# adaLN column sums turned by full transposes, and the final norm's weights transposed earlier, in a one-core hybrid layer

## The chip, the core and the metric

The kernel runs on one NeuronCore of a Trainium2 chip. The metric is device time in microseconds (us) of one execution. The engines named below are TensorE (PE in the profile, with its weight loads apart as PEld), VectorE (DVE), ScalarE (ACT), GpSimd (POOL) and the queue of SyncE (SP), which issues the weight transfers.

## What is computed

One decoder layer for 256 tokens of width 1024, in float32. A conditioning vector c gives nine rows of 1024 numbers (adaLN): shift, scale and gate for each of three sub-layers. The reference, cut to what matters here:

```python
ada = jax.nn.silu(c) @ w_ada[l] + b_ada[l]
sh1, sc1, g1, sh2, sc2, g2, sh3, sc3, g3 = jnp.split(ada, N_ADA, axis=-1)
h = modulate(rmsnorm(x, norm_ffn1[l]), sh1, sc1)
x = x + 0.5 * g1[:, None, :] * swiglu(h, w_ffn1_in[l], w_ffn1_out[l])
...
y_att = moba_attention(...)
y_ssm = s5_mixer(...)
x = x + g2[:, None, :] * (merged @ w_out[l])
h = modulate(rmsnorm(x, norm_ffn2[l]), sh3, sc3)
x = x + 0.5 * g3[:, None, :] * swiglu(h, w_ffn2_in[l], w_ffn2_out[l])
return rmsnorm(x, norm_final)
```

## The kernel before

Activations lie transposed (features on partitions). Each weight element is split in two fp32r parts: ACT casts the high part (`w_hi`, line 271), DVE subtracts it to get the low part (`w_lo`, line 279), and PE makes three passes for each product (lines 302 to 304, and 475 to 477 for the output projections). Weight tiles of 1 MB come through four `raw` buffers; `nextq` hands out the split halves in order and counts them in `state["q"]`, and four buffers of each part are in use (`NSPLIT`).

The work runs in stages: FFN1 (to about 236 us), the projections of the mixing block, attention and the state-space scan (to about 372 us), the output projection, FFN2 (from about 424 us), the final norm. In the attention stage, sixteen gate units of 24 matmuls each (banks 4 to 6, lines 302 to 304) are the filler between the narrow pieces: scores (`L1249`, `L1250`), softmax on DVE and ACT (`L1263`, `L1269`, `L1274`), the transposes of the probabilities (`L1283`), their copies on ACT (`L1285`, `L1286`), the product with v (`L1302`, `L1304`), the state-space output (`L1223`) and its gelu on ACT (`L1234`). ACT loads one function table for gelu and another for the exponential.

The adaLN rows 2 to 8 of the nine (rows 0 and 1 go another way) are summed on DVE, as weight tiles arrive, into an accumulator of 128 x 1024, `acc` (line 251). When one is complete, `ada_done` puts a closure in the queue `pe_fill`; `fill`, called at fixed points of the stages, takes the first entry when `state["q"]` has reached its number. The closure sums over partitions with ones (`L378`, four products of 32 columns' weights, each quarter of the row then standing in 32 equal partitions), copies the 128 x 256 result to `ada_rows` (ACT, `L383`), turns it into columns on PE (`L385`) and adds bias on DVE (`ada_cols`). The seven closures run in the trace at 110.9, 154.8, 195.6, 287.9, 339.3, 372.0 and 550.2 us.

The weights of the final norm (8 x 128) are turned into columns by `final_gain` (`L1415` on PE, `L1416` on DVE), also from `pe_fill`; they are used only in the last stage, from 605.7 us. The order of instructions within an engine is set by a scheduler from the program and its own estimates, except in sections where the order is written out by hand.

Of the kernel before, what the change touches and what calls it, by code (L numbers as in the profile page):

```python
# [14 lines left out]
ALU = mybir.AluOpType  # L15
# [4 lines left out]
KD = D // 128  # L20
# [35 lines left out]
def kernel(ctx, tc, T, out):  # L56
    nc = tc.nc
# [33 lines left out]
    def bank(i):  # L91
        return psum.tile([128, 512], F32, tag=f"bank{i}", name=f"bank{i}")

    def sb(tag, shape, dt=F32, bufs=1, name=None):
        return parts[place.get(tag, "pool")].tile(shape, dt, tag=tag, name=name or tag, bufs=bufs)
# [127 lines left out]
    state = {"loaded": 0, "split": 0, "q": 0, "bank": 3}  # L223
# [4 lines left out]
    pe_fill = deque()  # L228
# [102 lines left out]
    ident = const.tile([128, 128], F32, name="ident")  # L331
# [9 lines left out]
    bada = cols0[:, 0:72].rearrange("p (v k) -> p v k", k=KD)  # L341
    ldt = const.tile([128, 16], F32, name="ldt")
    norm_cols = {1: cols0[:, 72:80], 4: cols[:, 32:40], 7: cols[:, 40:48]}
# [15 lines left out]
    ada = {v: const.tile([128, KD], F32, name=f"ada{v}") for v in range(9)}  # L359

    def ada_cols(v, p, ks):

        o, b = ada[v][:, ks], bada[:, v, ks]
        if v in norm_cols:
            nc.vector.scalar_tensor_tensor(out=o, in0=p, scalar=1.0, in1=b, op0=ALU.add, op1=ALU.add)
            nc.vector.tensor_tensor(out=o, in0=o, in1=norm_cols[v][:, ks], op=ALU.mult)
        else:
            nc.vector.tensor_tensor(out=o, in0=p, in1=b, op=ALU.add)
            if v % 3 == 2:
                nc.vector.tensor_scalar(o, o, 0.5, None, op0=ALU.mult)  # L370

    def ada_done(v):
        a = acc.pop(v)

        def do_cols():
            p = bank(state["bank"])
            for q in range(4):
                nc.tensor.matmul(  # L378
                    p[32 * q:32 * q + 32, 0:256], ones[:, 0:32], a[:, q * 256:(q + 1) * 256], start=True, stop=True,
                    tile_position=(0, 32 * q),  # L380
                )
            rs = sb("ada_rows", [128, 256])
            nc.scalar.copy(rs, p[:, 0:256])  # L383
            for n in range(2):
                nc.tensor.matmul(  # L385
                    p[:, 256 + n:264:2], rs[:, n * 128:(n + 1) * 128], ident[:, ::32], start=True, stop=True
                )
            ada_cols(v, p[:, 256:264], slice(0, KD))

        pe_fill.append((state["q"] + FILL_DELAY, do_cols))  # L390

# [16 lines left out]
    def ada_block_cols(b):  # L408
        a = block_sb.pop(b)
        p = bank(7)  # L410
        for n in range(2):
            nc.tensor.matmul(p[:, n:n + 1], a[:, n * 128:(n + 1) * 128], one1, start=True, stop=True)
        ks = slice(b, b + 1)
        ada_cols(1, p[:, 0:1], ks)
        ada_cols(0, p[:, 1:2], ks)
# [588 lines left out]
    start = ExitStack()  # L1004
# [26 lines left out]
    for j in range(1, 4):  # L1031
# [19 lines left out]
        out=sel, in_=sel, compare_op=ALU.is_equal, fill=0.0, base=0, pattern=[[-1, 2], [0, 64]], channel_multiplier=1  # L1051
# [93 lines left out]
    for j in range(4):  # L1145
        p = bank(4 + j)[:, 0:S]
# [3 lines left out]
        for n in range(4):  # L1150
            for t in range(4):
                o = U[32 * t:32 * t + 32, 4 * j + n, 1:NC4 + 1]
# [167 lines left out]
    for hd in range(8):  # L1320
        n = 2 * hd - (hd > 6)
# [11 lines left out]
    for n in range(16):  # L1333
        g, j = divmod(n, 8)
        p = bank(4 + n % 3)[:, 0:S]
# [34 lines left out]
    for q in range(4):  # L1370
        p = bank(4 + q)
# [7 lines left out]
    for q in range(4):  # L1379
        p = bank(4 + q)  # L1380
# [22 lines left out]
    ks = range(KD - HOLD, KD)  # L1403
# [11 lines left out]
        nc.tensor.transpose(p[:, 0:KD], rows[0], ident[0:8, 0:8])  # L1415
        nc.vector.tensor_copy(nf, p[:, 0:KD])  # L1416

    pe_fill.append((state["q"] + 30, final_gain))

    def each(g):  # L1420
        if g == 0:
# [37 lines left out]
    for t in range(2):  # L1459
        o = sb(("ssm_Pr", "ssm_Pi")[t], [128, D])  # L1460
# [37 lines left out]
```

## Time and profile before

| | us |
|---|---|
| median of 3 runs | 624.38 |
| lowest and highest of them | 622.92, 624.68 |
| profiled execution, its own time | 622.35 |
| its span, first to last instruction | 620.3 |
| PE busy | 601.8 (97%) |
| DVE busy | 456.6 (74%) |
| ACT busy | 327.5 (53%) |

The time of an execution is 2.05 us longer than its span. Busy time of PE counts pipelined matmuls, so two facts are read apart: how long PE had nothing to do, and the distance from the start of one matmul to the start of the next, which is what an instruction costs in a full stream.

### The profile page before, as it was taken

Reading aid. Unit: us, or ns where it says so; the run is one execution under the profiler, and the core shown is the slowest. Engines: PE = TensorE matmul, PEld = TensorE weight load, DVE = VectorE, ACT = ScalarE, POOL = GpSimd, SP = SyncE. Lnnn points to the kernel's source line nnn. Section 1 sums busy time; section 2 is a strip of 40 time slices with the busy share of each in tenths; the row PEclk is TensorE's granted clock in tenths of the full one; section 3 lists DMA queues with packets and bytes.
Section 4 is the critical chain, followed back from the end, with each engine's and each line's share of the span. In section 5 each row is a group of like instructions: output and inputs, shape, how many; then the busy total and the mean of one; then the engine's idle time right before and its main releaser. Section 6 shows DMA issues by size and latency. Waiting matters only on the chain.

```text
span 620.3 us, 12787 instructions
## 1 busy us (share of the span) xinstructions
PE 601.8 (97%) x5328; PEld 573.4 (92%) x5328; DVE 456.6 (74%) x838; ACT 327.5 (53%) x537; POOL 23.6 (4%) x37
## 2 busy tenths in 40 slices
PE   7999999999999998999999999997999999999996
PEld 6778999999999998998877899997999999999995
DVE  2699999899875577999998758865984646654533
ACT  5336856488434453756446865454744344434434
POOL 5200000020000001000000000001000000000000
PEclk9999999999999997999999999997999999999997
DMA  9999989866887645698337745574376755855301
GB/s 277 333 253 330 340 281 326 291 233 231 273 288 251 205 136 186 225 313 295 138 137 278 267 136 204 173 235 135 139 261 213 248 170 195 272 175 170 132 2 69
DMA packets 97706, 136.70 MB, mean 220 GB/s; under 512 B 7697, under 2 KB 77410, under 8 KB 97648
## 3 DMA queue, kind: packets, MB, share of 16 engines
q1 hardware_dynamic: 97360, 135.81, 65.7%
q8 instruction: 42, 0.69, 0.5%
q14 instruction: 16, 0.13, 0.1%
q0 software_dynamic: 288, 0.07, 0.1%
HBM read 134.82 MB, written 1.05 MB: 219 GB/s over the span
## 4 chain that ended last, share of the span: by engine, by line
PE 86%; DVE 7%; DMA 3%; ACT 1%; issue 1%; SPq 0%; POOLq 0%; DVEq 0%; ACTq 0%
PE bank L302 17%; PE bank L304 16%; PE bank L303 16%; PE bank L475 8%; PE bank L476 8%; PE bank L477 8%; PE bank L626 4%; DVE w_lo L279 2%; DMA raw<-in_w_ffn_in_dram 2%; DMA raw<-in_w_ada_dram 1%; PE bank L1223 1%; DVE ssm_U L1157 1%; PE bank L502 1%; PE bank L400 1%; DVE a L689 1%
## 5 line engine op out<-in xcount | busy, mean ns | idle before, releaser
L279 DVE TENSOR_TENSOR w_lo<-raw,w_hi 128x1024 fp32r<-128x1024 f32 (+1 forms) x184 | 221.4, 1210 | 90.7 <-ACT w_hi L271 90.2
L271 ACT CAST w_hi<-raw 128x1024 fp32r<-128x1024 f32 (+1 forms) x184 | 189.3, 1039 | 176.4 <-PE bank L303 106.3
L302 PE MATMUL bank<-h_hi,w_hi 128*128 128x256 f32 x736 | 208.2, 283 | 0.0
L304 PE MATMUL bank<-h_hi,w_lo 128*128 128x256 f32 x736 | 206.1, 280 | 0.8 <-DVE w_lo L279 0.7
L303 PE MATMUL bank<-h_lo,w_hi 128*128 128x256 f32 x736 | 205.9, 280 | 0.0
L302 PEld LDWEIGHTS bank<-h_hi,w_hi 128*128 128x128 f32 x736 | 138.6, 188 | 4.7 <-issue 2.8
L304 PEld LDWEIGHTS bank<-h_hi,w_lo 128*128 128x128 f32 x736 | 138.8, 189 | 1.7 <-DVE w_lo L279 1.1
L303 PEld LDWEIGHTS bank<-h_lo,w_hi 128*128 128x128 f32 x736 | 138.7, 188 | 0.1
L475 PE MATMUL bank<-a,w_hi 128*128 128x256 f32 x352 | 99.1, 282 | 0.0
L476 PE MATMUL bank<-a,w_hi 128*128 128x256 f32 x352 | 98.7, 280 | 0.0
L477 PE MATMUL bank<-a,w_lo 128*128 128x256 f32 x352 | 98.5, 280 | 0.0
L251 DVE SCALAR_TENSOR_TENSOR acc<-raw,csil,acc 128x1024 f32<-128x1024 f32 x49 | 62.7, 1280 | 7.8 <-DMA raw<-in_w_ada_dram 7.4
L475 PEld LDWEIGHTS bank<-a,w_hi 128*128 128x128 f32 x352 | 66.3, 188 | 1.0 <-issue 1.0
L477 PEld LDWEIGHTS bank<-a,w_lo 128*128 128x128 f32 x352 | 66.6, 189 | 0.0
L476 PEld LDWEIGHTS bank<-a,w_hi 128*128 128x128 f32 x352 | 66.4, 189 | 0.0
L302 PE MATMUL bank<-a,w_hi 128*128 128x258 f32 x128 | 38.8, 303 | 2.1 <-ACT w_hi L271 2.1
L303 PE MATMUL bank<-a,w_hi 128*128 128x258 f32 x128 | 38.2, 298 | 0.0
L304 PE MATMUL bank<-a,w_lo 128*128 128x258 f32 x128 | 37.2, 293 | 0.0
L626 PE MATMUL bank<-h_hi,w_hi 128*128 128x256 f32 x112 | 27.4, 292 | 1.2 <-ACT h_hi L452 0.8
L302 PEld LDWEIGHTS bank<-a,w_hi 128*128 128x128 f32 x128 | 26.0, 203 | 2.5 <-ACT w_hi L271 2.5
L626 PE MATMUL bank<-h_lo,w_hi 128*128 128x256 f32 x112 | 27.5, 284 | 0.0
L626 PE MATMUL bank<-h_hi,w_lo 128*128 128x256 f32 x112 | 27.3, 282 | 0.0
(323 smaller groups left out, 827.4 us busy)
## 6 DMA issues: line engine op xcount, KB each, us to landing
raw<-in_w_ffn_in_dram SPq DMA_DIRECT2D x36, 1024.0 KB, 5.2
raw<-in_w_ada_dram SPq DMA_DIRECT2D x28, 1024.0 KB, 5.3
raw<-in_w_ffn_out_dram SPq DMA_DIRECT2D x22, 1024.0 KB, 5.1
raw<-in_w_in_dram SPq DMA_DIRECT2D x16, 1024.0 KB, 6.4
raw<-in_w_ada_dram SPq DMA_DIRECT2D x16, 512.0 KB, 8.3
raw<-in_w_ffn_in_dram SPq DMA_DIRECT2D x8, 896.0 KB, 7.3
raw<-in_w_out_dram SPq DMA_DIRECT2D x4, 1024.0 KB, 4.9
raw<-in_w_br_att_dram SPq DMA_DIRECT2D x2, 1024.0 KB, 5.0
```

What stands on the lines that cost most here:

```text
L251: nc.vector.scalar_tensor_tensor(out=a, in0=r[:, k, :], scalar=cs, in1=a, op0=ALU.mult, op1=ALU.add)
L271: nc.scalar.copy(hi, r)
L279: nc.vector.tensor_tensor(out=lo, in0=r, in1=hi.bitcast(F32), op=ALU.subtract)
L302: nc.tensor.matmul(o, st[0], mv[0], start=first, stop=False)
L303: nc.tensor.matmul(o, st[0], mv[1], start=False, stop=False)
L304: nc.tensor.matmul(o, st[1], mv[0], start=False, stop=last)
L400: nc.tensor.matmul(p[q:q + 32, 0:256], csil[:, k, :], r[:, k, :], start=(k < 4), stop=(k >= 4), tile_position=(0, q))
L475: nc.tensor.matmul(mm3_o, wj[0], a[0], start=first and j % 2 == 0, stop=False)
L476: nc.tensor.matmul(mm3_o, wj[0], a[1], start=False, stop=False)
L477: nc.tensor.matmul(mm3_o, wj[1], a[0], start=False, stop=last and j % 2 == 1)
L502: nc.tensor.matmul(p[:, t:t + 1], z[:, t * 128:(t + 1) * 128], one1, start=(first and n == 0 and t == 0), stop=(last and n == len(parts) - ...
L626: nc.tensor.matmul(pb[b][:, n * S:(n + 1) * S], z[:, b * 128:(b + 1) * 128], h[hl][:, kb, :], start=(kb == 0 and n == 0 and y == 0), stop= ...
```

## The change

The two products that turn `ada_rows` into columns are replaced. Before, each used `ada_rows` as the stationary 128 x 128 operand and every 32nd column of the identity as the moving one (4 columns), and wrote 4 interleaved columns. Now each is a transpose of 128 x 128, whose 128 columns go to the upper half of the bank, and `ada_cols` reads every 32nd of them. And the number at which `final_gain` may run goes from 30 to 10 halves after the start of FFN2.

```diff
     def ada_cols(v, p, ks):
 
-        o, b = ada[v][:, ks], bada[:, v, ks]
+        o, b, g = ada[v][:, ks], bada[:, v, ks], norm_cols[v][:, ks] if v in norm_cols else None
+        if len(p.shape) == 3:
+            o, b, g = (z if z is None else z.rearrange("p (q n) -> p q n", n=2) for z in (o, b, g))
         if v in norm_cols:
             nc.vector.scalar_tensor_tensor(out=o, in0=p, scalar=1.0, in1=b, op0=ALU.add, op1=ALU.add)
-            nc.vector.tensor_tensor(out=o, in0=o, in1=norm_cols[v][:, ks], op=ALU.mult)
+            nc.vector.tensor_tensor(out=o, in0=o, in1=g, op=ALU.mult)
...
             for n in range(2):
-                nc.tensor.matmul(
-                    p[:, 256 + n:264:2], rs[:, n * 128:(n + 1) * 128], ident[:, ::32], start=True, stop=True
-                )
-            ada_cols(v, p[:, 256:264], slice(0, KD))
+                nc.tensor.transpose(p[:, 256 + n * 128:384 + n * 128], rs[:, n * 128:(n + 1) * 128], ident)
+            ada_cols(v, p[:, 256:512].rearrange("p (n q c) -> p q n c", n=2, q=4)[:, :, :, 0], slice(0, KD))
...
-    pe_fill.append((state["q"] + 30, final_gain))
+    pe_fill.append((state["q"] + 10, final_gain))
```

The scheduler also places some instructions of the attention stage differently. On ACT, in the stretch from about 342 to 356 us of the trace before, the row stood thus (`a_4529` is the output of gelu, its two rows the two halves of the second block; `at_e` the exponentials of a head, two rows each):

```order
247 L1234 ACT_TABLE_LOAD
248 L1234 ACTIVATE a_4529<-bank_4215 128x4x64
249 L1255 ACTIVATE at_bias<-dist 128x256
250 L1234 ACTIVATE a_4529<-bank_4215 128x4x64
251 L1341 ACTIVATE ssm_G_3657<-bank_4422 128x256
252 L271 CAST w_hi<-raw 128x1024
253 L1269 ACT_TABLE_LOAD
254 L1269 ACTIVATE at_e,at_st<-a_3699,at_st 128x128
255 L1269 ACTIVATE at_e,at_st<-a_3699,at_st 128x256
```

Now, on the same engine, from the same first table load on:

```order
247 L1234 ACT_TABLE_LOAD
248 L1234 ACTIVATE a_4529<-bank_4215 128x4x64
249 L1269 ACT_TABLE_LOAD
250 L1269 ACTIVATE at_e,at_st<-a_3699,at_st 128x128
251 L1269 ACTIVATE at_e,at_st<-a_3699,at_st 128x256
```

And nine rows further on, still on ACT:

```order
260 L1234 ACT_TABLE_LOAD
261 L1234 ACTIVATE a_4529<-bank_4215 128x4x64
262 L1269 ACT_TABLE_LOAD
263 L1269 ACTIVATE at_e,at_st<-a_3699,at_st 128x128
264 L1269 ACTIVATE at_e,at_st<-a_3699,at_st 128x256
```

The second half of that gelu has moved behind the exponentials of one head more, and two table loads have been added.

On PE, the transposes of the probabilities of the head whose exponentials are the last two of these rows (`bank_4562`) stood in the gate unit `bank_4586` thus:

```order
2434 L302 MATMUL bank_4586<-h_hi,w_hi 128x256
2435 L1283 MATMUL bank_4562<-ident,at_e 128x128
2436 L303 MATMUL bank_4586<-h_lo,w_hi 128x256
2437 L1283 MATMUL bank_4562<-ident,at_e 128x128 x2
2438 L304 MATMUL bank_4586<-h_hi,w_lo 128x256
```

Now, in the same unit, which begins at row 2431:

```order
2444 L303 MATMUL bank_4586<-h_lo,w_hi 128x256
2445 L1283 MATMUL bank_4562<-ident,at_e 128x128
2446 L304 MATMUL bank_4586<-h_hi,w_lo 128x256
2447 L302 MATMUL bank_4586<-h_hi,w_hi 128x256
2448 L1283 MATMUL bank_4562<-ident,at_e 128x128 x2
2449 L303 MATMUL bank_4586<-h_lo,w_hi 128x256
```

They stand behind fourteen matmuls of the unit instead of one.

On PE, at the beginning of FFN2, behind the second output step (`L477`) and ahead of the first input step (`L302`, `h_hi`), the rows now are:

```order
3161 L476 MATMUL bank_5643<-a_5312,w_hi 128x256
3162 L477 MATMUL bank_5643<-a_5312,w_lo 128x256
3163 L1415 MATMUL bank_5702<-ident,rows_96 128x8
3164 L302 MATMUL bank_5705<-h_hi,w_hi 128x256
3165 L303 MATMUL bank_5705<-h_lo,w_hi 128x256
```

Before, `L477` and `L302` were neighbours there, and `L1415` stood some 480 rows later. The order of POOL and of the DMA queue is unchanged.

## Rows read from the trace of the kernel before

**Rows 1.** The page, part 4: the chain that ended last, by engine.

```profile
PE 86%; DVE 7%; DMA 3%; ACT 1%; issue 1%; SPq 0%; POOLq 0%; DVEq 0%; ACTq 0%
```

**Rows 2.** Stretches: length, busy us (count) of PE, PEld, DVE, ACT, POOL; clock, DMA.

```profile
100.00:200.00 100.00, 100.00 (x917) 98.05 (x916) 83.05 (x128) 56.50 (x80) 3.69 (x3) 1.00 0.78 273
338.00:364.00 26.00, 26.00 (x259) 21.85 (x259) 17.95 (x42) 18.84 (x46) 0.00 (x0) 1.00 0.58 207
440.00:613.00 173.00, 173.00 (x1483) 171.96 (x1482) 101.36 (x116) 78.55 (x98) 0.00 (x0) 1.00 0.53 177
```

**Rows 3.** Groups by line: busy us, mean ns of one record, idle before.

```profile
L385 PE MATMUL bank<-ident,ada_rows 128*128 128x4 f32 x28 | 3.7, 239 | 0.1
L887 PE MATMUL bank<-ident,big 128*128 128x128 f32 x32 | 4.9, 274 | 0.0
```

**Rows 4.** Timeline of PE at the first closure: start, us, instruction.

```profile
110.77 0.28 PE L304 MATMUL bank<-h_hi,w_lo 128*128 128x256 f32 x1
110.88 0.55 PE L385 MATMUL bank<-ident,ada_rows 128*128 128x4 f32 x4
111.29 0.36 PE L302 MATMUL bank<-h_hi,w_hi 128*128 128x256 f32 x1
111.49 0.28 PE L303 MATMUL bank<-h_lo,w_hi 128*128 128x256 f32 x1
111.61 0.28 PE L304 MATMUL bank<-h_hi,w_lo 128*128 128x256 f32 x1
```

**Rows 5.** Timeline of PE around four transposes of line 887.

```profile
99.72 0.28 PE L477 MATMUL bank<-a,w_lo 128*128 128x256 f32 x1
99.83 0.60 PE L887 MATMUL bank<-ident,big 128*128 128x128 f32 x4
100.19 0.37 PE L302 MATMUL bank<-h_hi,w_hi 128*128 128x256 f32 x1
100.40 0.28 PE L303 MATMUL bank<-h_lo,w_hi 128*128 128x256 f32 x1
```

**Rows 6.** Timeline of PE around two transposes of line 1283.

```profile
350.85 0.37 PE L302 MATMUL bank<-h_hi,w_hi 128*128 128x256 f32 x1
351.06 0.38 PE L1283 MATMUL bank<-ident,at_e 128*128 128x128 f32 x2
351.19 0.36 PE L303 MATMUL bank<-h_lo,w_hi 128*128 128x256 f32 x1
351.39 0.28 PE L304 MATMUL bank<-h_hi,w_lo 128*128 128x256 f32 x1
```

**Rows 7.** Timeline of PE after the fourth closure, with the waits.

```profile
293.00 0.28 PE L302 MATMUL bank<-h_hi,w_hi 128*128 128x256 f32 x1
293.71 0.52 PE L1165 MATMUL bank<-ssm_U,ssm_G 128*128 128x64 f32 x3 [0.43 <-DVE a L689]
...
312.53 0.39 PE L304 MATMUL bank<-h_hi,w_lo 128*128 128x256 f32 x1 [0.71 <-DVE w_lo L279]
```

**Rows 8.** Timeline of ACT from the second gelu to the next heads' exponentials.

```profile
345.12 0.62 ACT L1234 ACTIVATE a<-bank 128x256 f32<-128x256 f32 x1
346.32 0.38 ACT L1341 ACTIVATE ssm_G<-bank 128x256 f32<-128x256 f32 x1 [0.58 <-PE bank L304]
...
347.66 1.28 ACT L1269 ACT_TABLE_LOAD   x1
348.96 0.40 ACT L1269 ACTIVATE at_e<-a,at_st 128x128 f32<-128x128 f32 x1
...
353.74 0.40 ACT L1269 ACTIVATE at_e<-a,at_st 128x128 f32<-128x128 f32 x1 [0.57 <-DVE at_st L1267]
```

**Rows 9.** Line 1415: min/median/max ns, first and last start.

```profile
L1415 PE MATMUL bank<-ident,rows x1: 223/223/223, 507.5 to 507.5; 8*128 8x8 f32 x1
```

**Rows 10.** Timelines of DVE and of PE before the new place of line 1415.

```profile
447.83 0.15 DVE L1079 COPY rawc<-bank 128x1 f32<-128x1 f32 x1
...
450.78 0.28 PE L477 MATMUL bank<-a,w_lo 128*128 128x256 f32 x1
```

## The prediction

> **What bounds the kernel now.** I began with the chain that ended last: 86% of the span is PE's, 7% DVE's, 1% ACT's [rows 1]. An edit is therefore worth what it changes in PE's stream, as long as PE is the engine that is late in that stage. The table of stretches says where that holds: PE is without a gap from 100 to 200 us, from 338 to 364 and from 440 to 613, and in the last of these ACT and DVE are busy for 79 and 101 of 173 us [rows 2]. Six of the seven closures lie in such a stream (110.9, 154.8, 195.6, 339.3, 372.0, 550.2 us). The fourth, at 287.9 us, does not: 5 us after it, PE waits for the scan on DVE, its next matmul starting at 293.71 after one at 293.00, and at 312.53 it waits again, for a split weight that DVE owes [rows 7]. There DVE is late, and what PE saves is waited away.
>
> **What a product costs and what a transpose costs.** I read this from distances between starts, because the durations overlap. In a full stream one 256-column pass starts 0.12 us after the other [rows 4]. Around the first closure, the pass ahead of the two products starts at 110.77 and the second pass behind them at 111.49: 0.72 us, of which two ordinary steps are 0.24, so the pair of products costs 0.48 us. The trace has 28 records for 14 products [rows 3]: each runs twice, with a weight load for each run, four steps of about 0.11 us for a pair.
>
> No pair of transposes of this operand is in the trace, but transposes of the same shape and type are. Line 887 has 32 of them in the program and 32 records [rows 3], so each runs once. Four of them put 100.40 - 99.72 - 0.24 = 0.44 us into the stream [rows 5], which is 0.22 for two. Two transposes of line 1283, which stand one matmul behind a third, put in 351.39 - 350.85 - 0.24 = 0.30 [rows 6]. The new transposes come as a pair with nothing like it in front, as the four do, so I take 0.22 and keep 0.30 as the other bound. A place then saves 0.26 us, at least 0.18.
>
> The Trainium skill (TensorE: Matmul & The Clock Gate, section Back-to-back issue gap) would have it the other way: a warm matmul of 1 to 64 columns costs about 60 cycles and one of 128 columns 134, so fourteen transposes for fourteen narrow products would lose about 0.4 us by an estimate from that page. The trace does not bear this out, since the narrow product steps at 0.11 us per record and has two records.
>
> Six places at 0.18 to 0.26 give 1.1 to 1.6 us; I take 1.3, since the other clean places have slightly cheaper products than the first. With the fourth counted too, the upper bound is 1.8. A loss is excluded at these places as long as a transpose runs once.
>
> **The rest of the closure.** The four sums, the copy on ACT and the two or three small DVE instructions stay, with as many elements; the wider step with which DVE reads the bank touches 8 elements. A result that is some tenths earlier is used only a stage later. Nothing is counted.
>
> **The moved transpose of the norm's weights.** It is one matmul of 223 ns [rows 9] and one DVE copy of 8 columns in both versions, so only its new place can cost. In front of it PE needs bank 3, whose last reader in the first steps of FFN2 is a copy on DVE at 447.83, done by 447.98; PE comes to the place after 450.78 [rows 10]. There are 2.8 us of cover. The load of its input stands among the first on SP's queue, whose order does not change. On DVE the copy stands behind a 1.2 us subtraction that begins after the transpose is done, so DVE doesn't wait. If the cover went, PE would stand and with it the stream to the end, one for one; I count 0.
>
> **The scheduler's other moves.** This is the term I can bound but not read off. In 338 to 364 us ACT gets two more table loads. A load takes 1.28 us, and the exponential behind it starts at once: 347.66 plus 1.28 is 348.94, and it starts at 348.96 [rows 8]. So ACT gets 2.6 us more. It is busy 18.8 of these 26 us [rows 2], so its 7.2 us of waiting can hold the loads as a sum; the question is where. For one head the exponentials move forward, since the second gelu half (0.62), a wait of 0.58 and a cast no longer stand ahead of them. For the next head they have three things ahead of them that were elsewhere or not there: load, gelu half, load, 1.28 + 0.62 + 1.28 = 3.2 us. Before, those exponentials waited 0.57 us for DVE [rows 8], and the head before now frees ACT earlier, by something between 1 and 2 us. That leaves them 0.6 to 1.6 us late. Waiting for them is the head's transposes on PE, and those stand 13 matmuls later in the unit than before, 13 x 0.12 = 1.5 us. So PE waits 0 to 0.1 us here; the late head also pushes the last one, whose transposes stand 8 matmuls, or about 1 us, later. Bounds: PE may even gain some tenths, as fewer of its narrow pieces stand right behind their inputs, and may lose at most the 2.6 us of ACT. The row it is nearest to is the wait of 0.57, so I take a loss of 0.3.
>
> **Sum.** 622.35 (the profiled execution: span 620.3 and 2.05 around it) - 1.3 + 0 + 0.3 = 621.35, so 1.0 us less. The median of the runs shown, 624.38, lies 2.0 above that execution; the same 1.0 taken from it gives 623.4, which I predict. A change of under 0.3% (1.9 us) can hardly be told from none in this kernel, whose three runs alone spread over 1.8 us. So this forecast reads as the same time, slightly to the fast side.
>
> **Rivals.**
>
> *The reshuffle helps (622.0 and less).* All seven places save 0.26 (1.8 us) and PE's stream in the attention stage loses waits: narrow pieces of heads and scan stand later behind their inputs. For it: most of the moved rows on PE move back, which removes waits. Against it: PE shows no gap in 338 to 364 [rows 2], so there is little to win. It gives 624.4 - 2.4, about 622.0; less if the scan's wait of 0.43 and the one of 0.71 [rows 7] shrink as well.
>
> *The table loads land on PE (slower).* One mechanism: the exponentials of the head behind the two loads come later than 1.5 us after their old time, PE stands at the first transpose of that head, and in a stream in which PE is without a gap the wait goes to the end. It decides from the point where ACT's earlier start of that chain is under 1.1 us (3.2 - 0.57 - 1.5). At the full 2.6 us of the two loads the time is 624.4 - 1.3 + 2.6 = 625.7; with the moved gelu half too, 626.3, which is 0.3% slower. The Trainium skill (ScalarE: Activation LUTs, section What ACT_TABLE_LOAD costs) counts some 1.38 us of draining besides the 1283 ns of a load, which would double the price by an estimate; the exponential that starts 0.02 us behind the load [rows 8] shows no such time behind it.
>
> *A transpose is not cheaper here.* It would run twice like the product, or stall on the copy that feeds it. At 0.44 for a pair and with the same wait the places save nothing: 624.4 + 0.3 = 624.7. Against it stand the 32 records of 32 transposes [rows 3]. If a narrow product cost by its columns, next to nothing, two transposes (0.22) would come on top, and six places would lose 1.3 us at most. This is what the page of the Trainium skill named above amounts to.
>
> **How the numbers follow.** The forecast, with 1.9 us less to 0.6 us more, gets 0.55; the helpful reshuffle 0.20, most of it beyond 0.3%; the loads on PE 0.18, of which two thirds beyond 0.3%; the transpose without gain 0.07. This gives faster 0.23, same 0.62, slower 0.15. From the medians' side the forecast's own range is 622.5 to 625.0. For 8 in 10 I go to the middle of the helpful case and the upper end of the loads, and add the spread of the runs: 620.6 to 626.2.
>
> **What would show each step.** In the profile of the changed kernel, the transposes of the closures have 14 records instead of 28, and the distance over them is 0.22 to 0.30 plus two steps; if it is 0.44, the third rival holds. `L1415` stands near 450 us and its neighbours have no wait; a wait of PE for DVE there would refute the cover of 2.8 us. ACT shows two more table loads, and in 338 to 364 PE shows a wait of under 0.5 us at the head's transposes; over 1 us of waiting for ACT there means the second rival. PE starts FFN2's stream 0.5 to 1.5 us earlier and ends it about 1 us earlier. The prediction is wrong if the total moves by over 2 us, and then most likely through ACT in the attention stage.

## The result, and the profile after

The change made the kernel 0.9% faster: 618.31 us (median of four runs, 616.08 to 620.20) against 624.53 of the kernel before, a ratio of 0.991 with a 95% interval of 0.988 to 0.994. The forecast was 623.4, its range 620.6 to 626.2, so the result lies below the range. Two repeats on other occasions gave 0.9928 (0.9897 to 0.9959) and 0.9945 (0.9919 to 0.9971). The profiled execution has a span of 612.5 us, 7.8 less than before.

The parts that were costed came out as costed. The groups by line of the kernel after answer to [rows 3]: 14 records for 14 transposes, where 14 products had 28.

```profile
L387 PE MATMUL bank<-ident,ada_rows 128*128 128x128 f32 x14 | 2.7, 276 | 0.1
L887 PE MATMUL bank<-ident,big 128*128 128x128 f32 x32 | 4.9, 276 | 0.2 <-DVE ada L370 0.2
```

The timeline of PE at the first closure answers to [rows 4]: start, duration, instruction.

```profile
111.89 0.28 PE L304 MATMUL bank<-h_hi,w_lo 128*128 128x256 f32 x1
112.01 0.38 PE L387 MATMUL bank<-ident,ada_rows 128*128 128x128 f32 x2
112.14 0.36 PE L302 MATMUL bank<-h_hi,w_hi 128*128 128x256 f32 x1
112.34 0.28 PE L303 MATMUL bank<-h_lo,w_hi 128*128 128x256 f32 x1
```

From the pass ahead to the second pass behind are 112.34 - 111.89 = 0.45 us, less two steps of 0.24: the pair costs 0.21 where it cost 0.48. Read the same way at all six clean places, and without rounding, a pair costs 0.22 after and 0.44 to 0.49 before, which is 1.5 us for the six; the prediction took 1.3.

The gain is elsewhere. The next two fences give the marks of the program on PE, once for the kernel before and once for the kernel after: the sums of the second, third, sixth and seventh closure (`L378` before, `L380` after), the small products of a norm's sums that open the mixing block and FFN2 (`L502`), and the first products of the scan (`L1165`); the times are those of the first and the last start of each group.

```profile
L378 PE MATMUL bank<-acc,ones x8: 379/391/403, 153.4 to 153.6; 128*32 128x256 f32 x8
L378 PE MATMUL bank<-acc,ones x8: 379/391/403, 194.1 to 194.4; 128*32 128x256 f32 x8
L502 PE MATMUL bank<-ones,h_lo x8: 352/352/372, 235.8 to 237.4; 128*128 128x1 f32 x8
L1165 PE MATMUL bank<-ssm_U,ssm_G x32: 217/275/294, 278.9 to 282.5; 128*128 128x64 f32 x32
L378 PE MATMUL bank<-acc,ones x8: 379/391/403, 363.0 to 363.3; 128*32 128x256 f32 x8
L502 PE MATMUL bank<-ones,h_lo x8: 352/352/372, 424.2 to 425.7; 128*128 128x1 f32 x8
L378 PE MATMUL bank<-acc,ones x8: 379/391/403, 548.7 to 549.0; 128*32 128x256 f32 x8
```

```profile
L380 PE MATMUL bank<-acc,ones x8: 379/391/403, 154.7 to 155.0; 128*32 128x256 f32 x8
L380 PE MATMUL bank<-acc,ones x8: 379/391/403, 193.8 to 194.1; 128*32 128x256 f32 x8
L502 PE MATMUL bank<-ones,h_lo x8: 250/250/271, 235.3 to 236.1; 128*128 128x1 f32 x8
L1165 PE MATMUL bank<-ssm_U,ssm_G x32: 217/275/294, 276.9 to 280.6; 128*128 128x64 f32 x32
L380 PE MATMUL bank<-acc,ones x8: 379/391/403, 360.1 to 360.4; 128*32 128x256 f32 x8
L502 PE MATMUL bank<-ones,h_lo x8: 250/250/353, 419.7 to 420.6; 128*128 128x1 f32 x8
L380 PE MATMUL bank<-acc,ones x8: 379/391/403, 541.3 to 541.5; 128*32 128x256 f32 x8
```

With the scan's late start (293.71 in [rows 7], 291.77 in the row shown further down) the spans divide so:

| from - to | before | after | difference |
|---|---|---|---|
| start - closure 2 | 153.4 | 154.7 | +1.3 |
| closure 2 - closure 3 | 40.7 | 39.1 | -1.6 |
| closure 3 - first `L502` | 41.7 | 41.5 | -0.2 |
| first `L502` - first `L1165` | 43.1 | 41.6 | -1.5 |
| first `L1165` - late start of the scan | 14.8 | 14.9 | +0.1 |
| late start of the scan - closure 6 | 69.3 | 68.3 | -1.0 |
| closure 6 - second `L502` | 61.2 | 59.6 | -1.6 |
| second `L502` - closure 7 | 124.5 | 121.6 | -2.9 |
| closure 7 - end of the span | 71.6 | 71.2 | -0.4 |

The second, seventh and eighth of these lines hold one closure or one small transpose each, and none of them could bring over 0.3 us by the prediction's prices. What shrank there is the ordinary stream, and in the eighth also a stretch of lower clock (see "What is not the change's"). The table of stretches counts PE's matmuls in windows in which nothing runs but 256-column passes; first before, then after (length, busy us and count, granted clock, DMA share, GB/s).

```profile
168.00:190.00 22.00, 22.00 (x189) 1.00 0.80 274
385.00:410.00 25.00, 25.00 (x215) 1.00 0.72 243
455.00:500.00 45.00, 45.00 (x384) 1.00 0.71 238
512.00:540.00 28.00, 28.00 (x250) 1.00 0.70 229
560.00:595.00 35.00, 35.00 (x300) 1.00 0.36 121
```

```profile
168.00:190.00 22.00, 22.00 (x197) 1.00 0.78 267
385.00:410.00 25.00, 25.00 (x223) 1.00 0.71 233
455.00:500.00 45.00, 45.00 (x399) 1.00 0.71 239
512.00:540.00 28.00, 28.00 (x249) 1.00 0.70 232
560.00:595.00 35.00, 35.00 (x299) 1.00 0.26 90
```

PE is busy all the time, at the full granted clock (the level of 2.4 GHz), in both, and yet gets through 4% more passes in three of the windows. (A count takes in some two passes that only overlap a window's ends.) The starts show two steady paces: behind the second closure 327 steps take from 155.41 to 193.92 us before, 117.8 ns each, and from 156.52 to 193.59 after, 113.3 each. Whichever holds after an interruption of the stream is kept until the next one. Before, the fast pace stood behind `L1415`, from 508 to 549 us, and not in front of it. After, it stands behind the new place of `L1415` (446 to 541 us), and behind the second and the sixth closure.

The chain that ended last, by engine, answers to [rows 1]: PE's share is down from 86 to 76%, DVE's up from 7 to 15. PE is now more often just behind DVE; its waits for DVE, by the table of waits, grew only from 6.3 to 7.5 us in all.

```profile
PE 76%; DVE 15%; DMA 3%; ACT 2%; issue 2%; SPq 0%; POOLq 0%; DVEq 0%; ACTq 0%
```

So the account by pace, at 4.4 ns per pass: 327 behind the second closure, 1.4 us; some 350 behind the sixth, 1.5; 480 between the two places of `L1415`, 2.1. Together 5.0 of the 7.8 us. (In the trace before, the new place lies at 450.8 us, behind the last line of [rows 10]; 446 us is its time in the kernel after. The expectations below count from 446 in the trace before, and so say 526 passes and 2.3 us.) The cheaper pairs add 1.5 and the attention stage 0.7 to 0.8, both told below. That is 7.2 us, while the medians moved by 6.2, and by 4.5 and 3.4 in the two repeats. One possible reason, not tested by time: in some executions the kernel before has the fast pace behind its third and seventh closure too (some 250 and 460 passes, 3.1 us), which the kernel after had there in none of three traces.

### The profile page after: what moved, and what is told of

Its sections match the earlier page's. It is cut to its first block, busy times and chain, and to the rows that moved or that the text cites. A ratio compares the mean times of both kernels' runs of the same rounds, so it can differ in the third digit from the quotient of the medians.

```text
span 612.5 us, 12760 instructions
## 1 busy us (share of the span) xinstructions
PE 593.6 (97%) x5314; PEld 566.2 (92%) x5314; DVE 456.3 (74%) x838; ACT 329.8 (54%) x539; POOL 23.4 (4%) x37
## 4 chain that ended last, share of the span: by engine, by line
PE 76%; DVE 15%; DMA 3%; ACT 2%; issue 2%; SPq 0%; POOLq 0%; DVEq 0%; ACTq 0%
PE bank L302 15%; PE bank L304 14%; PE bank L303 14%; PE bank L475 7%; PE bank L476 7%; PE bank L477 7%; DVE w_lo L279 5%; PE bank L626 4%; DVE acc L251 3%; DMA raw<-in_w_ada_dram 2%; DVE a L689 2%; PE bank L400 1%; PE bank L1223 1%; DVE ssm_U L1157 1%; ACT w_hi L271 1%
## 5 line engine op out<-in xcount | busy, mean ns | idle before, releaser
L302 PE MATMUL bank<-h_hi,w_hi 128*128 128x256 f32 x736 | 207.1, 282 | 0.0
L302 PEld LDWEIGHTS bank<-h_hi,w_hi 128*128 128x128 f32 x736 | 138.1, 188 | 4.6 <-issue 3.3
L477 PE MATMUL bank<-a,w_lo 128*128 128x256 f32 x352 | 98.1, 279 | 0.0
L477 PEld LDWEIGHTS bank<-a,w_lo 128*128 128x128 f32 x352 | 66.2, 188 | 0.0
L302 PE MATMUL bank<-a,w_hi 128*128 128x258 f32 x128 | 38.4, 300 | 2.1 <-ACT w_hi L271 2.1
L302 PEld LDWEIGHTS bank<-a,w_hi 128*128 128x128 f32 x128 | 25.6, 200 | 2.6 <-ACT w_hi L271 2.5
```

Source lines behind the costliest of these rows:

```text
L302: nc.tensor.matmul(o, st[0], mv[0], start=first, stop=False)
L477: nc.tensor.matmul(mm3_o, wj[1], a[0], start=False, stop=last and j % 2 == 1)
```

## The experiments

Ratios are to the kernel before, run in turn with each kernel on the same chip. Before against itself (e5, e15) came out at 1.0006 and 1.0028, so a ratio here is good to about 0.3%. The last five columns are counts of PE's matmuls, by the table of stretches, in windows behind the second, third and sixth closure (168 to 190, 206 to 221, 385 to 410 us), behind the new place of `L1415` (455 to 500) and behind the seventh closure (560 to 595). The slow pace gives 189, 130, 215, 384 and 300; the fast one 197, 135, 223, 400 and 311.

| kernel | median us | ratio (95% interval) | 2nd | 3rd | 6th | FFN2 | 7th |
|---|---|---|---|---|---|---|---|
| before, first trace | | | 189 | 130 | 215 | 384 | 300 |
| e5 before again | 624.12 | 1.0006 (0.9977-1.0035) | 189 | 134 | 214 | 384 | 311 |
| e15 before, third trace | 625.80 | 1.0028 (0.9997-1.0058) | 189 | 130 | 215 | 384 | 300 |
| after, first trace | 618.31 | 0.9910 (0.9882-0.9938) | 197 | 130 | 223 | 399 | 299 |
| e6 after again | 619.62 | 0.9928 (0.9897-0.9959) | 197 | 130 | 223 | 400 | 299 |
| e12 after, third trace | 618.28 | 0.9945 (0.9919-0.9971) | 197 | 130 | 223 | 399 | 299 |
| e1 `L1415` moved only | 619.71 | 0.9958 (0.9935-0.9981) | 189 | 135 | 214 | 400 | 299 |
| e2 transposes only | 619.95 | 0.9964 (0.9939-0.9989) | 196 | 129 | 223 | 385 | 300 |
| e9 transposes at 2 and 6 | 621.14 | 0.9999 (0.9967-1.0031) | 196 | 130 | 223 | 384 | 300 |
| e10 transposes at the other five | 623.18 | 1.0023 (0.9997-1.0049) | 189 | 135 | 214 | 385 | 300 |
| e13 as e9, `L1415` moved | 619.60 | 0.9932 (0.9897-0.9966) | 196 | 129 | 223 | 400 | 311 |
| e3 before, small transposes | 620.18 | 0.9976 (0.9950-1.0002) | 197 | 135 | 223 | 400 | 299 |
| e4 after, small transposes | 621.27 | 0.9976 (0.9950-1.0001) | 189 | 134 | 223 | 400 | 299 |
| e7 after, two alone | 619.20 | 0.9918 (0.9887-0.9949) | 186 | 130 | 222 | 399 | 300 |
| e8 before, four alone | 627.21 | 1.0058 (1.0031-1.0084) | 196 | 135 | 223 | 400 | 300 |
| e11 after, 3 and 7 later | 614.55 | 0.9894 (0.9856-0.9932) | 192 | 129 | 223 | 399 | 311 |
| e14 the same again | 618.49 | 0.9914 (0.9880-0.9948) | 196 | 130 | 223 | 400 | 300 |

**One part alone.** e1 is the kernel before with

```diff
-    pe_fill.append((state["q"] + 30, final_gain))
+    pe_fill.append((state["q"] + 10, final_gain))
```

> The kernel before, with only the final norm's transpose (L1415) moved to the first steps of FFN2; the narrow products stay. Theory 1, pace: an interruption of PE's stream of 256-column passes decides whether the passes behind it step at 113 or at 118 ns; L1415 is one after which they step at 113, so the 526 passes between 446 and 507 us become 4.4 ns shorter each. The time falls by 2.3 us (ratio about 0.996), and the distances between starts from 446 to 507 us fall from 117.8 to 113.3 ns. Theory 2, the prediction's reckoning: the move is worth 0, the ratio lies within 0.999 to 1.001, and the pace there stays at 117.8 ns; the whole gain then comes from the transposes and the attention stage.

It is 0.42% faster, 2.6 us, the fast pace is there (400), and a ratio of 1 lies outside the interval. That the move is free of waits was right; that it is worth nothing was not. e2 is the kernel after with that line undone.

> The changed kernel with L1415 back at its old place, so the transposes alone (with the scheduler's moves in the attention stage). Theory 1, pace: cheaper pairs give 1.5 us, and the passes behind the second and the sixth closure (325 and about 350 of them, 4.4 ns each) give 3.0 more, with about 1 us out of the attention stage: 4.5 to 5.5 us less than before (ratio 0.991 to 0.993), while the stretch from 446 to 507 us is back at 117.8 ns per pass. If the pace is drawn anew in each build or run, the 3.0 us may be missing, and then the records show those stretches at 117.8. Theory 2, the prediction's reckoning: 1.0 to 1.3 us less (0.998), with no stretch of ordinary passes changed.

Both paces came as expected; the time, 0.36% less, is less than the 0.7 to 0.9% expected, and the interval does not reach that, though it is clear of none. e1 and e2 together, 0.78%, are about the whole change (0.55 to 0.90%).

**Repeats for the paces** (no edit).

> The kernel before, unchanged, for a second trace. Theory 1, the pace is set by the kind and place of the interruption: the passes behind the second, sixth and seventh closure and from 446 to 507 us step at 117.8 ns again, and those from 508 to 549 us at 113.3. Theory 2, the pace is drawn anew at each execution: at least one of these long stretches (325, 359, 467, 526 and 356 passes) shows the other pace. The time is that of before either way (ratio 0.997 to 1.003).

> The changed kernel, unchanged, for a second trace and for its time on the same chip as the others. Theory 1, the pace is set by the kind and place of the interruption: 113.3 ns behind the second and sixth closure and from 446 to 541 us, 117.8 behind the third and seventh, as in its first trace. Theory 2, the pace is drawn anew: at least one of these is the other way round. The ratio to before is 0.989 to 0.994 by the first result; 0.994 to 0.997 if the moved transpose and the cheaper pairs are all that lasts.

> The changed kernel once more, for its time on the chip of the three kernels above. Theory 1: a third trace has 113.3 ns behind the second and sixth closure and from 446 to 541 us, and 117.8 behind the third and seventh, as the first two; ratio 0.990 to 0.993. If the pace is drawn anew at each execution, one of these places differs.

> The kernel before for a third trace. Theory 1: 117.8 ns behind the second and sixth closure and from 446 to 507 us, as in two traces; behind the third and seventh either pace (one of each in the two). The ratio is 0.997 to 1.003.

The places that carry the gain are fixed: in three traces each, 189 and 215 before, 197 and 223 after, 384 against 399, all within one. The third and the seventh closure with narrow products are not: e5 is the kernel before, to the letter, with the fast pace behind both.

**Which closures bring it.** e9 has full transposes at two closures, e10 at the other five, `L1415` at its old place in both:

```diff
+            if v in (4, 6):
+                for n in range(2):
+                    nc.tensor.transpose(p[:, 256 + n * 128:384 + n * 128], rs[:, n * 128:(n + 1) * 128], ident)
...
+            else:
+                for n in range(2):
+                    nc.tensor.matmul(
+                        p[:, 256 + n:264:2], rs[:, n * 128:(n + 1) * 128], ident[:, ::32], start=True, stop=True
+                    )
...
```

e10 has `v not in (4, 6)` instead; each branch ends in the `ada_cols` that fits it.

> The kernel before, with the two full transposes at the second and the sixth closure only, the narrow products at the other five, and L1415 at its old place. In four traces with transposes the passes behind these two closures stepped at 113.3 ns every time, in four with narrow products at 117.8 every time. Theory 1, pace: 325 and about 350 passes become 4.4 ns shorter, 3.0 us, and two cheaper pairs 0.5: 3.5 us faster than before (ratio 0.993 to 0.996). Theory 2, work alone: 0.5 us faster (0.999).

> The counterpart: full transposes at the other five closures, narrow products at the second and the sixth, L1415 at its old place. Behind the third and the seventh closure (264 and 467 passes) four traces with transposes show 117.8 ns every time, four with narrow products 113.3 in two of the four. Theory 1, pace: on the mean 1.6 us are lost there, against 1.0 of cheaper pairs: 0 to 1 us slower than before (ratio 1.000 to 1.002). Theory 2, work alone: 1.0 to 1.3 us faster (0.998).

> The kernel before with the full transposes at the second and sixth closure only, and L1415 moved; none of the scheduler's moves in the attention stage. Theory 1, pace: 113.3 ns behind these two closures (3.0 us) and from 446 to 541 us (2.3 us), two cheaper pairs 0.5: 5 to 6 us faster than before (ratio 0.990 to 0.993), about as much as the whole change less one microsecond for the attention stage. If the trace shows these paces and the time stays within 0.3% of before, as it did for the two closures alone, then pace in the traces does not carry into the time, and theory 1 falls.

The pace goes with the closure's instruction, place by place (196 and 223 in e9, 189 and 214 in e10), whatever the other closures do. By time, e10 with its five cheaper pairs is not the 0.2% faster that work alone would make it, and e9 with two is 2.0 us faster than e10, where work alone would have it slower. Against before, e9 shows nothing (0.9999), and its interval ends just short of the 0.993 to 0.996 expected: by time alone, the gain behind these two closures is not shown. e13, which adds the move to it, is 0.68% faster, and its interval takes in what was expected. The size of a pace's gain is read from the traces, and the times bear it out only to some 0.3%.

**Trying to set the pace.** e3 (before) and e4 (after) add a small transpose behind the pair in each closure, of the shape of `L1415`; nothing reads it.

```diff
+            nc.tensor.transpose(p[:, 264:272], rs[0:8, 0:128], ident[0:8, 0:8])    # e4: p[:, 0:8]
```

> The kernel before, with one small transpose (8 rows of 128 columns, of L1415's shape) added behind the two narrow products in each of the seven closures; its result is used by nothing. Theory 1, pace: PE has more to do, and yet the passes behind the closures that stepped at 117.8 ns (325, 257, 359 and 467 of them) step at 113.3, which gives back 6.2 us, less 0.1 to 0.35 for each of seven transposes: 4 to 5.5 us faster than before (ratio 0.991 to 0.994). Theory 2, only the instructions of the closures count: 0.7 to 2.4 us slower (1.001 to 1.004).

> The changed kernel with the same small transpose added behind the two full ones in each closure. Theory 1, pace: the passes behind the third and the seventh closure (264 and 467), which still step at 117.8 ns in the changed kernel, step at 113.3: 3.2 us less, minus 0.7 to 2 us for seven transposes, so 1 to 2.5 us faster than the changed kernel (some 8 to 10 us faster than before, ratio 0.984 to 0.987). Theory 2, only the instructions of the closures count: 0.7 to 2.4 us slower than the changed kernel.

In e3 the pace turned fast behind the second, third and sixth closure, narrow products and all, and stayed slow behind the seventh. With more work the kernel is 0.24% faster, where 0.6 to 0.9% was expected and where work alone would have made it slower; the interval just reaches none. In e4 it turned fast behind the third and slow behind the second, where the pair alone had been fast, and nothing is gained over the kernel after (0.9976, where 0.984 to 0.987 was expected). The rule "a small transpose makes it fast" falls. (In e3, and in e8 below, the window of FFN2 is fast although `L1415` stands at its old place behind it, so it is not the only thing that can make it so.) e7 (after) and e8 (before) put it alone into the stream, 17 to 23 passes later:

```diff
+            if v in (3, 8): pe_fill.appendleft((state["q"] + 1, lambda: nc.tensor.transpose(p[:, 0:8], ident[0:8], ident[0:8, 0:8])))    # e8: v in (4, 3, 6, 8)
```

> The changed kernel with two small transposes more (8 rows of 128 columns, used by nothing), each alone in the stream like L1415, some 16 passes behind the third and the seventh closure. Theory 1, pace: a small transpose that stands alone leaves 113.3 ns behind it, so 264 and 450 passes become 4.4 ns shorter: 3.2 us less for 0.5 us of added work, 2.7 us faster than the changed kernel (ratio to before 0.985 to 0.988). Theory 2, what counts is work: 0.5 us slower than the changed kernel.

> The kernel before, narrow products and all, with four such small transposes alone in the stream, some 16 passes behind the second, third, sixth and seventh closure. Theory 1, pace: about 310, 245, 340 and 450 passes become 4.4 ns shorter, 6.0 us less for four times 0.24 us of added work, so about 5 us faster than before (ratio 0.991 to 0.993) without any of the change's edits. Theory 2, what counts is work: 1 us slower (1.001 to 1.002).

In e7 both stretches stayed slow (130, 300), and its 0.9918 is the changed kernel's time. In e8 the passes turned fast behind three closures, but the kernel got slower: the added transpose at the second closure writes a bank that DVE has yet to read, and PE stood. The timeline of PE in e8, with the wait:

```profile
160.86 0.28 PE L304 MATMUL bank<-h_hi,w_lo 128*128 128x256 f32 x1
163.47 0.27 PE L389 MATMUL bank<-ident 8*128 8x8 f32 x1 [2.33 <-DVE ada L365]
163.67 0.58 PE L475 MATMUL bank<-a,w_hi 128*128 128x256 f32 x1
164.05 0.41 PE L476 MATMUL bank<-a,w_hi 128*128 128x256 f32 x1
```

After the wait of 2.33 us the passes step at 0.21 us, up to 166.8, in a stretch of half the granted clock (a mean of 0.50 from 163.5 to 166.8). That price hides what the paces gave, so the time of e8 decides between neither theory. In e7 a fast pace also met another limit: DVE's low parts come too late for it once, at 186.18, in the window that counts 186:

```profile
186.18 0.39 PE L304 MATMUL bank<-h_hi,w_lo 128*128 128x256 f32 x1 [0.64 <-DVE w_lo L279]
```

**A later place.** e11, and e14 again, run the third and the seventh closure of the changed kernel 24 passes later; no instruction is added.

```diff
-        pe_fill.append((state["q"] + FILL_DELAY, do_cols))
+        pe_fill.append((state["q"] + FILL_DELAY + (v in (3, 8)), do_cols))
```

> The changed kernel with the third and the seventh closure one weight half (24 passes) later, so that the pair of transposes is followed by a pass of line 303 (an input step), as at the second and sixth closure, and not by one of line 476 (an output step). No instruction is added or removed. Theory 1, the pace behind a pair depends on the instructions around it: 113.3 ns behind all four long places, about 240 and 440 passes 4.4 ns shorter, 3.0 us faster than the changed kernel (ratio to before 0.986 to 0.989). Theory 1b, the pace depends on the place in the program in another way: 117.8 ns stays behind these two. Theory 2, work alone: the time of the changed kernel (0.991 to 0.993).

> The changed kernel with the third and seventh closure one weight half later, once more. Theory 1: 113.3 ns behind the second, sixth and seventh closure, 117.8 behind the third, as in its first trace; 2.0 us faster than the changed kernel at the seventh closure, ratio to before 0.986 to 0.991. If the pace there is drawn anew at each execution, the seventh shows 117.8 and the time is that of the changed kernel (0.991 to 0.994).

e11 had the fast pace behind the seventh closure and is the fastest kernel here, 614.55 us where e12 on the same chip took 618.28. Its repeat had the slow pace there, and 0.9914, which is the changed kernel's. So the later place is no worse, and not shown to be better; behind the third closure it changed nothing. (The 192 of e11 behind the second closure is the fast pace too, with four longer steps of 0.20 to 0.34 us.)

## Why the prediction was wrong

**The chain and the cover held.** PE bounds the stages that shrank, and its saving reached the end. `L1415` ran at 445.69 without a wait in front of it, so the cover held.

```profile
445.48 0.28 PE L477 MATMUL bank<-a,w_lo 128*128 128x256 f32 x1
445.69 0.22 PE L1415 MATMUL bank<-ident,rows 8*128 8x8 f32 x1
445.84 0.38 PE L302 MATMUL bank<-h_hi,w_hi 128*128 128x256 f32 x1
```

**A pair at 0.22 instead of 0.48: right**, 0.21 at the first closure, and the term was 1.5 us where 1.3 was taken. By the table of the Trainium skill (TensorE: Matmul & The Clock Gate, section Back-to-back issue gap), which gives a single matmul by itself, the transposes would have cost more than the narrow products; in this stream they do not, with 0.21 against 0.48 us for a pair.

**The fourth place: right.** The time from the first `L1165` to its late start stayed at 14.8 to 14.9 us; PE came to that instruction earlier and waited longer, 0.93 us where [rows 7] have 0.43. The row of the kernel after:

```profile
291.77 0.96 PE L1165 MATMUL bank<-ssm_U,ssm_G 128*128 128x64 f32 x7 [0.93 <-DVE a L689]
```

**The step that failed is the price of the ordinary stream.** The prediction read 0.12 us per pass from [rows 4] and took it for a constant, so that an edit could only be worth its own instructions. The step has two values, 113.3 and 117.8 ns, and an interruption chooses between them for hundreds of passes. With it fails the sentence "I count 0" for the moved `L1415`: its own cost is the same in both places, but 480 passes behind it became 4.4 ns shorter, 2.1 us by trace and 2.6 by time (e1). The same holds for the second and the sixth closure, 3 us by trace; by time this part is not shown on its own (e9). The rows of before had it: in the windows shown above, 384 passes in 45 us ahead of the old place of `L1415` are 117 ns each, 250 in 28 us behind it 112 (both with the two at the ends).

**The scheduler's other moves: wrong in sign.** They were counted as a loss of 0.3, with a gain of some tenths as the bound. The stage from the scan's late start to the sixth closure is 1.0 us shorter, of which the cheaper pair of the fifth closure is 0.2 to 0.3. The 0.7 to 0.8 that are left belong to the moves: nine traces with them have 68.2 to 68.7 us for this stage, eight without (before, e1, e3, e5, e8, e9, e13, e15) 69.2 to 69.6. The moves and the cheap fifth pair stand in the same nine traces, so the times alone do not part them; the record of PE does, as told below. The two more table loads are there, and PE waits for neither. The timeline of ACT:

```profile
341.14 1.28 ACT L1234 ACT_TABLE_LOAD   x1
342.44 0.65 ACT L1234 ACTIVATE a<-bank 128x256 f32<-128x256 f32 x1
343.09 1.28 ACT L1269 ACT_TABLE_LOAD   x1
344.38 0.40 ACT L1269 ACTIVATE at_e<-a,at_st 128x128 f32<-128x128 f32 x1
```

Here too the exponential starts right behind its load (343.09 + 1.28 = 344.37, and it starts at 344.38), and the load right behind the gelu (342.44 + 0.65 = 343.09). The draining time that the Trainium skill adds to a load (ScalarE: Activation LUTs, section What ACT_TABLE_LOAD costs) does not show on either side of it. What PE gained is in its own order. Before, three transposes of the probabilities were split over the state-space products:

```profile
340.23 0.28 PE L304 MATMUL bank<-h_hi,w_lo 128*128 128x256 f32 x1
340.44 0.30 PE L1283 MATMUL bank<-ident,at_e 128*128 128x128 f32 x1
340.67 0.30 PE L1223 MATMUL bank<-a,big 128*32 128x64 f32 x2
340.90 0.44 PE L1283 MATMUL bank<-ident,at_e 128*128 128x128 f32 x2
341.27 0.37 PE L1223 MATMUL bank<-a,big 128*32 128x64 f32 x11
```

After, they stand together behind one pass:

```profile
340.06 0.49 PE L1283 MATMUL bank<-ident,at_e 128*128 128x128 f32 x3
340.30 0.36 PE L303 MATMUL bank<-h_lo,w_hi 128*128 128x256 f32 x1
340.50 0.28 PE L304 MATMUL bank<-h_hi,w_lo 128*128 128x256 f32 x1
```

From 340.44 to 341.27 are 0.83 us for the three and two small products, against 0.24 up to the next pass when the three stand together. Between the fifth and the sixth closure PE runs the same instructions in both kernels, the pair aside. By the distances from start to start in its timeline, the steps within one kind sum to 18.7 us before and 18.8 after, and one pass behind another takes 125 ns there on the mean in both, so this is not the pace; the steps from one kind of instruction to another sum to 6.6 us before (39 of them) and 5.6 after (36). Of this 1.0 us the stretch ahead of the fifth closure, with two passes more, gives back 0.2. The prediction looked for waits here, found none, and so found "little to win"; changes between kinds of instruction cost PE time without any wait.

**What is not the change's.** Two of the stages go with stretches of half the granted clock (the level of 1.2 GHz) around the two `L502`. The table of stretches there has the clock in the column ahead of the DMA share; first the kernel before, then the kernel after, then the kernel after in its third trace (e12).

```profile
230.00:250.00 20.00, 17.83 (x117) 17.02 (x117) 15.45 (x23) 8.10 (x12) 1.65 (x1) 0.83 0.53 175
418.00:436.00 18.00, 14.52 (x99) 14.22 (x99) 10.88 (x24) 8.65 (x12) 1.62 (x1) 0.81 0.37 117
```

```profile
230.00:250.00 20.00, 17.52 (x128) 16.81 (x127) 16.69 (x27) 8.99 (x14) 1.65 (x1) 0.91 0.62 212
418.00:436.00 18.00, 16.26 (x122) 16.20 (x122) 12.72 (x27) 9.11 (x14) 1.61 (x1) 0.91 0.39 121
```

```profile
230.00:250.00 20.00, 17.53 (x114) 16.82 (x113) 15.15 (x21) 7.89 (x12) 1.65 (x1) 0.83 0.56 184
418.00:436.00 18.00, 14.52 (x100) 14.31 (x99) 11.98 (x24) 8.47 (x12) 1.61 (x1) 0.81 0.36 117
```

The same kernel has 0.91 in one execution and 0.83 and 0.81 in another. From the first `L502` to `L1165` PE takes 41.6 to 41.9 us in the seven traces that have 0.91 there, and 42.9 to 43.5 in the ten that have 0.83, whatever the kernel. From the second `L502` to the seventh closure the kernel after takes 121.6 us, and 121.5 in e6, with 0.91, but 122.5 in e12. So the whole of the -1.5, and some 0.9 of the -2.9, is luck of the execution; the 2.0 that is left of the latter is the pace's 2.1.

The 1.3 us at the start are not the change's either. From 0 to 20 us the mean clock is 0.83 in the kernel after and 1.00 in the kernel before, but that this is the reason is not shown: e12 has 1.00 there and still reaches the second closure at 155.1 us. Three traces of the kernel before reach it at 153.4 to 157.1, three of the kernel after at 154.7 to 159.7. Such differences may be one reason why the ratios of the changed kernel lie between 0.991 and 0.9945; this was not tested.

**Open.** What makes an interruption leave one pace or the other. It is not work, and not the clock, which is 1.00 in every one of these windows. It is not the share of DMA: behind the seventh closure the fast pace stands with 0.44 (e5), 0.29 (e13) and 0.27 (e11), the slow one with 0.26 (after) to 0.44 (e8). It is not the shape alone: `L1415` left the fast pace in all 17 traces (in e3, e4, e8 and e13 it was fast ahead of it already), while a transpose of the same shape alone in the stream left it slow twice in e7, and fast three times and slow once in e8. Behind the second and sixth closure the pair gave the fast pace in nine traces of nine and the narrow products the slow one in five of five (before, e1, e5, e10, e15; e3, e4 and e8, with small transposes added, aside). Behind the third and the seventh the narrow products gave either, and the pair the fast one once in place (e10, third) and once 24 passes later (e11, seventh).

## What to carry to other kernels

In a stream in which one engine never waits, read the distance between starts on both sides of every interruption before costing an edit to the interruption: a few per cent of hundreds of instructions outweigh the edit. Such a gain is real but fragile, so measure it at each place and more than once, and try another kind or place of the interrupting instruction before doing more work on its length. Transposes and small products that stood together cost less here than scattered ones, though no wait showed in either case. And before the difference of two traces is shared out among causes, a second and third trace of the same kernel show which stages differ by themselves.

## What the runs showed of the hardware

- A stream of 256-column passes with a weight load each has two steady paces at the full granted clock, 113.3 and 117.8 ns from start to start, kept for up to 860 passes (e11, e14); it changes only where other instructions interrupt the stream.
- The same program can take the other pace at the same place in another execution (e5, 134 and 311 against 130 and 300), while behind the second and the sixth closure and in FFN2 each of the two kernels kept its pace in three traces.
- The stretch of half the granted clock between the stages shows as a mean of 0.91 or 0.83 from 230 to 250 us, for one and the same kernel, and costs some 1.0 to 1.9 us more in the second case (42.9 to 43.5 us against 41.6 to 41.9, in 17 traces).
- In a full stream a pair of 128x128 transposes costs 0.22 us, and a pair of products with 4 columns, each of which runs twice, 0.44 to 0.49.
- Steps from one kind of instruction to another cost PE time without a recorded wait: 39 of them 6.6 us before, 36 of them 5.6 us after, from the fifth to the sixth closure.
